# A bias added by a matmul, routing placed ahead of gate 2 on TensorE, and GpSimd splitting three of four weight quarters

## Chip, core and metric

One core of a Trainium2 chip runs the whole kernel. The metric is device time in microseconds of one launch. The kernel before took 1426.2 us (median of 3 runs, 1423.9 to 1431.74).

## What is computed

One layer of an encoder with 256 tokens of width 2048, all in float32. Its weights are read once: 539 MB in all. Cut to its steps:

```python
c_act = jax.nn.silu(c)
mod = c_act @ w_ada[l] + b_ada[l]
sh1, sc1, g1, sh2, sc2, g2 = [m[:, None, :] for m in jnp.split(mod, 6, axis=-1)]
h = rms_norm(x, g_mix[l]) * (1 + sc1) + sh1
y = token_mixer(h, w_in[l], ..., w_out[l])      # gMLP, pooling, attention; ends with @ w_out
x = x + g1 * y
h = rms_norm(x, g_ffn[l]) * (1 + sc2) + sh2
x = x + g2 * moe_ffn(h, w_router, b_router, e_gate[l], e_up[l], e_down[l])

def moe_ffn(h, ...):                            # 16 experts, top-1 group, top-2 experts
    eidx, gw = route(ht, w_router, b_router)
    order = jnp.argsort(flat_e)                 # tokens sorted by expert
    hid = jax.nn.silu(xb @ w_gate[e]) * (xb @ w_up[e])
    return hid @ w_down[e]                      # weighted by the gate, summed per token
```

## The kernel before

The program is written as one list of steps, without a scheduler: each engine runs its instructions in the order in which they stand in the code, and waits only for the data and buffers that it needs.

**Stages.** First come the mixer's projections. `w_in` is taken in five chunks of rows (`CHUNKS`; the last three have four blocks of 128 rows), each chunk in nine pieces of 512 columns. Then 16 tiles of `w_out` in four column groups `n` (`wout_steps`, `x1_block`). Then the routing of the tokens, the gather of the normalised tokens into `XT` (16 blocks, four matmuls each), and the experts, 15 of which are visited in `ORDER`, with 8 tiles of `e_gu` and 4 of `e_down` for each, 2 MB a tile.

**Loads.** All weights come through SyncE's DMA queue (SP) into a ring of four 2 MB tiles (`ring` three times, `ringm`), which are used as eight halves of 1 MB until the experts begin. Two more (`ringl`) take the place of the buffers `xhl` and `oneh` when the gather has read them (`s_phl.close()`). SP issues in the order of the code; a load waits for the last reader of its buffer.

**Splitting.** A quarter of a `w_in` or `w_out` tile (128x512) is split into a high part, which ScalarE casts, and a low part, which VectorE ("V") or GpSimd ("G") computes by a subtraction (`split`, L176). `WSPLIT` and `WSO` name the engine of each quarter. TensorE then takes six matmuls for a quarter (`mm3` for each half of the tokens), the third of which is the first to need the low part. Up to six quarters lie ready (`LOOK_SPLITS`).

**Modulation rows.** A row such as gate 2 (`g2`, section 5 of `w_ada`) is computed in four parts of 512 columns. Each part takes four 1 MB tiles; `ada_parts` accumulates them on TensorE in rows 0, 32, 64 and 96 of one PSUM bank (`accs[0]`), four matmuls a tile. A step waits in the list `todo`, so its load is issued some steps ahead of its matmuls (`LOOK` = 4, a gate-2 step counts 2). At the end of a part `gate_row` copies the bank to `r2[q]` on ScalarE (L795) and adds the bias in one row on VectorE (L797). Of the 16 gate-2 steps five are issued among the last `w_out` tiles (`G2`), one behind them (`G2_MID`), and the others by two calls of `g2_run`: one ahead of the routing's counts, one behind the matmul that gives the experts' order.

**Routing.** `M` marks the two experts of each token (L1050). `pp` holds the sums over tokens, by matmuls of `M` (L1056 to L1061). From them VectorE makes `key`, a rank, and the one-hot `ohc`; the matmul `po` (L1087) turns it into the order of the experts; `irow` (L1091) is that order as integers. SP reads `irow` before it can issue the first expert's load (L1352). `x_lo` (L1004) is the low part of the normalised tokens, four instructions of VectorE that the gather needs but the order doesn't. `oneh` (L1118) is the one-hot matrix by which the gather's matmuls sort the tokens. `g2w` (L1187 to L1190) spreads gate 2 over all partitions, by four matmuls with `sel`; the expert stage needs it.

## Time and profile before

| | |
|---|---|
| time, three runs | 1423.9, 1426.2, 1431.74 us |
| profiled execution | 1423.43 us, span 1421.7 us, mean granted TensorE clock 0.959 |
| TensorE matmul (PE) busy | 1202.6 us, 85% of the span, 6638 instructions |
| VectorE (DVE) busy | 628.1 us, 44%, 1168 |
| ScalarE (ACT) busy | 363.7 us, 26%, 661 |
| GpSimd (POOL) busy | 161.1 us, 11%, 127 |
| DMA | 539.13 MB, mean 379 GB/s |

Times in the views count from the start of the span. PE is TensorE's matmul row and PEld its weight loads; matmuls overlap in the records, so the distance from one start to the next tells their rate, and the recorded length of a single one does not. A float32 matmul stands as two instructions. The granted clock is given as a share of 2.4 GHz: 0.50 is the lower level, 1.2 GHz. "Idle before" in brackets names what ended an engine's wait. The time beyond the span, 1423.43 - 1421.7 = 1.7 us, is the same start and end in every run and is left as it is.

### The profile page before, as it was taken

To read this page: it belongs to the slowest core of one execution; us is meant where nothing else is said; L and a number is where in the kernel's file an instruction comes from. 1 tells how busy PE (TensorE), PEld (TensorE's weight loads), DVE (VectorE), ACT (ScalarE), POOL (GpSimd) and SP (SyncE) were. 2 spreads that over 40 slices of the span, in tenths; PEclk is the share of its full clock that TensorE was granted. 3 is DMA by queue.
4 is the path that set the end of the run, shared out by engine and by line. 5 is a ranking of instruction groups with operands and counts; after the bars stand their busy time and mean duration, and the time that the engine had idled before them with its cause. 6 is when DMAs were issued, how large, how long until landed. Compare 5 with 4: busy or idle time off the path is not lost.

```text
span 1421.7 us, 17020 instructions
## 1 busy us (share of the span) xinstructions
PE 1202.6 (85%) x6638; PEld 625.6 (44%) x6638; DVE 628.1 (44%) x1168; ACT 363.7 (26%) x661; POOL 161.1 (11%) x127
## 2 busy tenths in 40 slices
PE   5998999999899686899968999688885888858865
PEld 3665676665676252664325743322232222322221
DVE  4366585765786463893327951121130211302112
ACT  4543334535444240771005820000000000000000
POOL 1333433321444000000000000000000000000000
PEclk9999999999999888999989999999998999989988
DMA  9888686899979489998999989999999999999997
GB/s 391 355 349 317 248 349 228 322 342 354 366 293 379 176 355 428 426 427 334 427 426 427 427 331 429 426 427 427 426 427 426 427 427 427 426 426 427 427 427 291
DMA packets 49222, 539.13 MB, mean 379 GB/s; under 512 B 5472, under 2 KB 5600, under 8 KB 7024
## 3 DMA queue, kind: packets, MB, share of 16 engines
q1 hardware_dynamic: 47664, 534.79, 91.6%
q10 hardware_dynamic: 1472, 3.19, 0.6%
q8 instruction: 54, 0.88, 0.2%
q14 instruction: 32, 0.26, 0.1%
HBM read 535.86 MB, written 2.10 MB: 378 GB/s over the span
## 4 chain that ended last, share of the span: by engine, by line
PE 33%; DMA 33%; DVE 2%; ACT 1%; issue 1%; DVEq 0%; ACTq 0%
PE lbank L171 24%; DMA ring<-in_e_down_dram 14%; DMA ring<-in_e_gu_dram 9%; DMA ringm<-in_e_gu_dram 6%; PE bank L171 4%; PE pm L171 3%; PE ada L171 2%; DMA ringl<-in_e_down_dram 2%; DMA ringl<-in_e_gu_dram 2%; DVE el L176 0%; DVE xhl L1004 0%; ACT xhl L998 0%; ACT el L175 0%; PE pt L171 0%; PE pt L892 0%
## 5 line engine op out<-in xcount | busy, mean ns | idle before, releaser
L171 PE MATMUL pm<-whl,hT 128*128 128x512 f32 x1056 | 283.2, 404 | 6.6 <-ACT whl L175 3.8
L171 PEld LDWEIGHTS pm<-whl,hT 128*128 128x128 f32 x1056 | 198.5, 192 | 78.7 <-issue 13.6
L171 PE MATMUL lbank<-ring,xr 128*32 128x256 f32 (+1 forms) x1216 | 155.4, 494 | 41.3 <-DMA ring<-in_e_gu_dram 41.3
L176 POOL TENSOR_TENSOR whl<-ring,whl 128x512 fp32r<-128x512 f32 x86 | 120.7, 1415 | 221.5 <-ACT whl L175 207.2
L171 PE MATMUL bank<-y,gt 128*128 128x512 f32 x240 | 119.9, 623 | 0.0
L175 ACT CAST whl<-ring 128x512 fp32r<-128x512 f32 x172 | 99.5, 621 | 64.8 <-PE pm L171 52.3
L1344 DVE TENSOR_TENSOR xa<-xa,bank 128x512 f32<-128x512 f32 x120 | 82.5, 688 | 73.6 <-PE bank L171 73.6
L171 PEld LDWEIGHTS lbank<-ring,xr 128*32 128x32 f32 (+1 forms) x1216 | 55.2, 127 | 133.6 <-issue 63.4
L1335 DVE TENSOR_TENSOR y<-lbank,g2w 128x512 f32<-128x512 f32 x60 | 41.5, 691 | 157.4 <-PE lbank L171 157.4
L171 PE MATMUL lbank<-ring,hidT 128*64 128x512 f32 (+1 forms) x416 | 81.7, 683 | 30.8 <-DVE hidT L1303 15.8
L171 PE MATMUL lbank<-ringl,xr 128*32 128x256 f32 (+1 forms) x608 | 80.3, 511 | 31.9 <-DMA ringl<-in_e_gu_dram 31.9
L176 DVE TENSOR_TENSOR whl<-ring,whl 128x512 fp32r<-128x512 f32 x86 | 84.6, 999 | 35.2 <-ACT whl L175 34.9
L171 PE MATMUL lbank<-el,xs 128*128 128x512 f32 x384 | 91.2, 395 | 7.3 <-ACT el L175 5.5
L1285 DVE TENSOR_TENSOR hid<-hid,lbank 128x512 f32<-128x512 f32 x11 | 7.6, 687 | 202.0 <-PE lbank L171 201.8
L171 PE MATMUL lbank<-ringm,xr 128*32 128x256 f32 (+1 forms) x608 | 78.4, 494 | 21.6 <-DMA ringm<-in_e_gu_dram 20.9
L1231 ACT COPY gt<-bank 128x256 f32<-128x256 f32 x15 | 5.6, 372 | 338.2 <-PE bank L1229 338.2
L171 PE MATMUL ada<-ring,cact 128*1 128x512 f32 (+1 forms) x568 | 70.4, 599 | 21.7 <-DMA ring<-in_w_ada_dram 13.1
L171 PEld LDWEIGHTS lbank<-el,xs 128*128 128x128 f32 x384 | 71.3, 188 | 27.4 <-ACT el L175 7.6
L171 PE MATMUL lbank<-ringl,hidT 128*64 128x512 f32 (+1 forms) x416 | 74.2, 598 | 4.7 <-DMA ringl<-in_e_down_dram 4.7
L171 PEld LDWEIGHTS bank<-y,gt 128*128 128x128 f32 x240 | 42.1, 193 | 73.3 <-issue 70.9
L454 DVE TENSOR_TENSOR z<-z,pm 128x512 f32<-128x512 f32 x72 | 48.5, 685 | 57.5 <-PE pm L171 57.5
L1280 DVE TENSOR_TENSOR hid<-hid,lbank 128x256 f32<-128x256 f32 x6 | 2.5, 421 | 158.8 <-PE lbank L171 136.3
(385 smaller groups left out, 1214.1 us busy)
## 6 DMA issues: line engine op xcount, KB each, us to landing
ring<-in_e_gu_dram SPq DMA_DIRECT2D x60, 2048.0 KB
ring<-in_w_ada_dram SPq DMA_DIRECT2D x79, 1024.0 KB, 6.9
ringm<-in_e_gu_dram SPq DMA_DIRECT2D x30, 2048.0 KB, 25.7
ringl<-in_e_gu_dram SPq DMA_DIRECT2D x30, 2048.0 KB, 24.9
ring<-in_e_down_dram SPq DMA_DIRECT2D x30, 2048.0 KB, 24.3
ringl<-in_e_down_dram SPq DMA_DIRECT2D x30, 2048.0 KB
ring<-in_w_in_dram SPq DMA_DIRECT2D x30, 1024.0 KB, 9.9
ring<-in_w_out_dram SPq DMA_DIRECT2D x12, 1024.0 KB, 7.9
```

The costliest lines, as they stand in the source:

```text
L171: E.matmul(out, lhsT=lhsT, rhs=rhs, start=start, stop=stop, skip_group_check=True)
L175: S.copy(hi, src)
L176: (eng or V).tensor_tensor(lo, src, hi.bitcast(F32), op=OP.subtract)
L454: V.tensor_tensor(dst, dst, P[h], op=OP.add)
L1231: S.copy(gt, p[:, :256])
L1280: V.tensor_tensor(hid[:, :256], hid[:, :256], P[1][:, :256], op=OP.mult)
L1285: V.tensor_tensor(hid[:, o], hid[:, o], P[2 * b + 1], op=OP.mult)
L1335: V.tensor_tensor(y, P, g2w[:, c0:c0 + 512], op=OP.mult)
L1344: V.tensor_tensor(a, a, p, op=OP.add)
```

## The change

Five edits belong together:

- The bias of gate 2 is added by a matmul: `bgt`, an 8x512 tile of both gates' biases, is multiplied with a one-hot column into row 0 of the part's bank. The part then ends with ScalarE's copy alone. The bias rows come by one DMA from ScalarE's queue in place of eight.
- The four parts of gate 2 alternate between `accs[0]` and `sets[0][0]`, a bank that the last column group of `w_out` doesn't use. The banks of `w_out` are named by `sets` in place of the rotation.
- Of the ten last gate-2 steps four, not eight, are issued ahead of the routing's counts. The other six, with the copies and `g2w`, come behind `oneh` in the code and ahead of the gather.
- One of the four `x_lo` stands ahead of `key`, and three behind `irow` (before: two and two).
- In the chunks 2, 3 and 4 of `w_in` and in `w_out` GpSimd splits the quarters 0, 2 and 3 and VectorE quarter 1 (before: V, G, V, G).

```diff
--- before.py
+++ after.py
@@ -64,10 +64,10 @@
 
 LAST = ["mwm", "mwm", "mw", "mawmam", "amw", "mmmwammm", "ammam", "ammammgmx", "amvammm", "aamsmapmtmmmm"]
 
-G2, G2_MID, NG2 = [1, 2, 1, 1], 1, 2
+G2, G2_MID, NG2 = [1, 2, 1, 1], 1, 4
 
 M1A, M1B, M2A, M2B, G1 = "PPVV", "PPPP", "PPPP", "PPPP", "PVVV"
-WSPLIT, WSO = ["VGVG"] * 5, "VGVG"
+WSPLIT, WSO = ["VGVG", "VGVG", "GVGG", "GVGG", "GVGG"], "GVGG"
 NORM = "GV"
 
 
@@ -255,8 +255,8 @@
         load_tile(w, wada_d, ADA[sec, k0, g])
         return w.rearrange("p (k n) -> p k n", n=n)
 
-    def ada_parts(sec, k0, nk, after, acc):
-        P = accs[acc]
+    def ada_parts(sec, k0, nk, after, acc, bias=None):
+        P = accs[acc] if isinstance(acc, int) else acc
         r = 16 // nk
         ng = KD // r
 
@@ -267,7 +267,10 @@
             def run(w):
                 for j in range(r):
                     k, t = r * g + j, j % 4
-                    mm(P[32 * t:32 * t + 1, :128 * nk], cact[:, k:k + 1], w[:, j, :], start=k < 4, stop=k >= KD - 4)
+                    mm(P[32 * t:32 * t + 1, :128 * nk], cact[:, k:k + 1], w[:, j, :], start=k < 4,
+                       stop=k >= KD - 4 and (t > 0 or bias is None))
+                if g == ng - 1 and bias is not None:
+                    mm(P[0:1, :], ident[0:8, bias:bias + 1], bgt, start=False)
                 if g == ng - 1:
                     after(P)
             return prep, run
@@ -791,13 +794,9 @@
     ss1 = cst.tile([128, 2, 4], F32, name="ss1")
     lnj = cst.tile([128, 1], F32, name="lnj")
 
-    def gate_row(sec, q, out, P):
+    def gate_row(out, P):
         S.copy(out, P)
-        o = slice(32 * q, 32 * q + 1)
-        V.tensor_tensor(out[o, :], out[o, :], bgr[o, sec // 3, :], op=OP.add)
-
-    def gate_args(sec, q, out):
-        return sec, 4 * q, 4, lambda P: gate_row(sec, q, out, P), 0
+        V.tensor_tensor(out[0:1, :], out[0:1, :], bgt[0:1, :], op=OP.add)
 
     wr = par("wr").rearrange("p (k e) -> p k e", e=16)
     wra = wk2.tile([128, KD, 16], F32, name="wra", bufs=1)
@@ -815,10 +814,8 @@
 
 
     rt, s_rt = pool("rt")
-    bgr = rt.tile([128, 2, 512], F32, name="bgr")
-    for q in range(4):
-        for a in range(2):
-            nc.scalar.dma_start(bgr[32 * q:32 * q + 1, a, :], bg_d[a:a + 1, 512 * q:512 * q + 512])
+    bgt = rt.tile([8, 512], F32, name="bgt2")
+    nc.scalar.dma_start(bgt, bg_d.rearrange("a (q n) -> (a q) n", n=512))
 
     def rtile(shape, name):
         return rt.tile(shape, F32, name=name)
@@ -857,7 +854,7 @@
     def wout_steps(n, Ps):
         def banks():
             if not Ps:
-                Ps.extend([pm(), pm()])
+                Ps.extend(sets[n % 2])
             return Ps
 
         def one(g):
@@ -907,7 +904,7 @@
 
     def g1_bc(n):
         p = pt()
-        mm(p, sel if n == 0 or G1[n] == "P" else ones, r4s[n])
+        mm(p, sel if n == 0 else ones, r4s[n])
         g1 = wk2.tile([128, 512], F32, name="g1")
         S.copy(g1, p)
         return g1
@@ -921,10 +918,8 @@
     def g1_steps(n):
         r4s.append(grow())
         if n == 0:
-            gate_row(2, 0, r4s[0], g1_first[0])
+            gate_row(r4s[0], g1_first[0])
             return []
-        if G1[n] == "P":
-            return steps(ada_parts(*gate_args(2, n, r4s[n])))
         return steps(sum_parts(2, 4 * n, 4, lambda a: None, 0, ENG(G1[n]), lambda: r4s[n], n))
 
     r4s = []
@@ -939,6 +934,7 @@
 
     g1_load(1)
     pbanks.append(accs[1])
+    sets = [list(pbanks)[:2], list(pbanks)[2:]]
     r2, g2p, g1s = [], deque(), {}
 
     def g2_run(n):
@@ -955,7 +951,8 @@
             if n == 3 and g == 0:
                 r2 += [grow2() for _ in range(4)]
                 for q in range(4):
-                    g2p.extend(ada_parts(*gate_args(5, q, r2[q])))
+                    g2p.extend(ada_parts(5, 4 * q, 4, lambda P, q=q: S.copy(r2[q], P), (accs[0], sets[0][0])[q % 2],
+                                         4 + q))
             if n == 3:
                 for _ in range(G2[g]):
                     step(*g2p.popleft())
@@ -1050,7 +1047,7 @@
     V.tensor_tensor(M, oh1, oh2, op=OP.add)
 
 
-    g2_run(len(g2p) - NG2)
+    g2_run(NG2)
     pp = pt()
     for h in range(2):
         mm(pp[:, 32:48], one2, M[:, h, :], h == 0, h == 1)
@@ -1059,7 +1056,7 @@
     mm(pp[:, 0:16], stri2, M[:, 0, :])
     mm(pp[:, 16:32], stri2, M[:, 1, :], stop=False)
     mm(pp[:, 16:32], one2, M[:, 0, :], start=False)
-    x_lo(2)
+    x_lo(1)
     SQ = [128, 16, 16]
     tmp = rtile(SQ, "tmp")
 
@@ -1085,11 +1082,9 @@
     V.tensor_scalar(ohc, ioE[0:16, 0, :], rkc[:, 16:17], None, op0=OP.is_equal)
     po = pt()
     mm(po[:, 0:16], ec.to_broadcast([16, 128]), ohc)
-    g2_run(16)
-    flush()
     irow = cst.tile([1, 128], I32, name="irow")
     V.tensor_copy(irow[:, 0:16], po[0:1, 0:16])
-    x_lo(2)
+    x_lo(3)
     order = rtile([128, 16], "order")
     V.tensor_copy(order, po[:, 0:16])
     pos = rtile([128, 3, 16], "pos")
@@ -1118,6 +1113,13 @@
         V.scalar_tensor_tensor(oneh[:, h, :], io512, sl2[:, 1, h:h + 1], oneh[:, h, :].bitcast(F32),
                                op0=OP.is_equal, op1=OP.add)
 
+    g2_run(16)
+    flush()
+
+    for b in range(4):
+        p = pm()
+        mm(p, sel, r2[b])
+        S.copy(g2w[:, 512 * b:512 * b + 512], p)
     def gather(k):
 
         p = pm()
@@ -1183,11 +1185,6 @@
         pick(gatO[:, h, :], ohO, gatR[:, h, :])
         V.tensor_tensor(posR[:, h, :], posR[:, h, :], dlt, op=OP.add)
 
-
-    for b in range(4):
-        p = pm()
-        mm(p, sel, r2[b])
-        S.copy(g2w[:, 512 * b:512 * b + 512], p)
     s_phl.close()
     pl, s_pl = pool("pl", 1, side="right")
     wides += [pl.tile([128, 2 * RINGW], F32, name=f"ringl{i}") for i in range(RING_LAST)]
```

The order of the loads on SP's queue is the same in both kernels. On GpSimd the number of split instructions grows from 104 to 147, and on VectorE it falls from 104 to 61: 27 tiles of `w_in` and 16 of `w_out`, one quarter each.

TensorE before, from the two tiles that stand ahead of `M`'s matmuls to the last gate-2 tile (`ada_113` is `accs[0]`, `pt_122` is `pp`, `pt_123` is `po`):

```order
L171 MATMUL ada_113<-ring_64,cact 1x512 x8
L171 MATMUL ada_113<-ring_65,cact 1x512 x4
L171 MATMUL ada_113<-ringm_2677,cact 1x512 x8
L171 MATMUL pt_122<-M,one_2710 128x16 x2
L171 MATMUL pt_122<-one_2710,M 16x1 x2
L171 MATMUL pt_122<-M,stri_2712 128x16 x2
L171 MATMUL pt_122<-M,one_2710 128x16
L171 MATMUL pt_123<-ohc,ec 128x16
L171 MATMUL ada_113<-ring_65,cact 1x512 x4
L171 MATMUL ada_113<-ring_63,cact 1x512 x8
L171 MATMUL ada_113<-ring_64,cact 1x512 x4
```

TensorE in the changed kernel at the same place (`pm_120` is `sets[0][0]`):

```order
L171 MATMUL pm_120<-ring_64,cact 1x512 x4
L171 MATMUL pm_120<-bgt_2689,ident 1x512
L171 MATMUL pt_122<-M,one_2703 128x16 x2
L171 MATMUL pt_122<-one_2703,M 16x1 x2
L171 MATMUL pt_122<-M,stri_2705 128x16 x2
L171 MATMUL pt_122<-M,one_2703 128x16
L171 MATMUL pt_123<-ohc,ec 128x16
L171 MATMUL ada_113<-ring_64,cact 1x512 x4
L171 MATMUL ada_113<-ring_65,cact 1x512 x4
L171 MATMUL ada_113<-ringm_2677,cact 1x512 x8
L171 MATMUL ada_113<-bgt_2689,ident 1x512
L171 MATMUL pm_120<-ring_65,cact 1x512 x4
```

Five tiles (20 matmuls) stood ahead of `pp` here, and now one; behind `po` there are eight tiles in place of four, and each part ends with a matmul of `bgt`.

TensorE before, at the end of the gather and the first expert's tile:

```order
L171 MATMUL pm_119<-oneh,xhl 128x512 x4
L171 MATMUL ada_114<-oneh,xhl 128x512 x4
L171 MATMUL pm_120<-grow_3327,sel 128x512
L171 MATMUL pm_121<-grow_3328,sel 128x512
L171 MATMUL pm_119<-grow_3329,sel 128x512
L171 MATMUL ada_114<-grow_3330,sel 128x512
L171 MATMUL lbank<-ringm_2677,xr_3910 32x256 x16
```

TensorE in the changed kernel, from the end of gate 2 to the first blocks of the gather:

```order
L171 MATMUL pm_120<-ring_64,cact 1x512 x4
L171 MATMUL pm_120<-bgt_2689,ident 1x512
L171 MATMUL pm_120<-grow_3320,sel 128x512
L171 MATMUL pm_121<-grow_3321,sel 128x512
L171 MATMUL pm_119<-grow_3322,sel 128x512
L171 MATMUL ada_114<-grow_3323,sel 128x512
L171 MATMUL pm_120<-oneh,xhl 128x512 x4
L171 MATMUL pm_121<-oneh,xhl 128x512 x4
```

The four matmuls of `g2w` stood between the gather and the first expert, and now stand ahead of the gather.

VectorE before, from `M` to the second pair of `x_lo` (`grow` is a row of `r2`, `xhl` is written by `x_lo`):

```order
L1050 TENSOR_TENSOR M<-oh_3608,oh_3615 128x32
L797 TENSOR_TENSOR grow_3328<-grow_3328,bgr 1x512
L797 TENSOR_TENSOR grow_3329<-grow_3329,bgr 1x512
L1004 SCALAR_TENSOR_TENSOR xhl<-xa,rs_3530,xhl 128x1024 x2
L1079 SCALAR_TENSOR_TENSOR key<-pt_122,rev 128x16
L1080 SCALAR_TENSOR_TENSOR keyc<-pt_122,revc 16x1
L1082 TENSOR_SCALAR rkc<-key,keyc 16x16
L1083 TENSOR_REDUCE rkc<-rkc 16x1
L1085 TENSOR_SCALAR ohc<-ioE,rkc 16x16
L797 TENSOR_TENSOR grow_3330<-grow_3330,bgr 1x512
L1091 CAST irow<-pt_123 1x16
L1004 SCALAR_TENSOR_TENSOR xhl<-xa,rs_3530,xhl 128x1024 x2
```

VectorE in the changed kernel:

```order
L1047 TENSOR_TENSOR M<-oh_3601,oh_3608 128x32
L1001 SCALAR_TENSOR_TENSOR xhl<-xa,rs_3523,xhl 128x1024
L1076 SCALAR_TENSOR_TENSOR key<-pt_122,rev 128x16
L1077 SCALAR_TENSOR_TENSOR keyc<-pt_122,revc 16x1
L1079 TENSOR_SCALAR rkc<-key,keyc 16x16
L1080 TENSOR_REDUCE rkc<-rkc 16x1
L1082 TENSOR_SCALAR ohc<-ioE,rkc 16x16
L1086 CAST irow<-pt_123 1x16
L1001 SCALAR_TENSOR_TENSOR xhl<-xa,rs_3523,xhl 128x1024 x3
```

Two bias additions left the way from `M` to `key`, and one left the place ahead of `irow`; one `x_lo` moved behind it.

## Rows read from the trace of the kernel before

**Rows 1.** Windows: length, busy of PE, PEld, DVE, ACT, POOL (counts), clock, DMA share, GB/s.
```profile
482.30:497.00 14.70, 9.01 (x68) 3.04 (x60) 5.57 (x11) 1.17 (x2) 0.00 (x0) 0.88 0.02 7
...
518.00:521.50 3.50, 3.50 (x16) 2.82 (x15) 3.04 (x11) 3.00 (x5) 0.00 (x0) 1.00 0.10 42
521.50:569.70 48.20, 35.25 (x344) 13.87 (x342) 13.00 (x26) 5.03 (x8) 0.00 (x0) 0.89 0.99 411
569.70:705.00 135.30, 126.62 (x527) 74.04 (x528) 82.61 (x137) 61.84 (x103) 0.00 (x0) 1.00 0.97 402
```

**Rows 2.** Chain that ended last, in order of time: start, length, what, count.
```profile
479.45 4.96 PE ada L171 x32
...
485.75 2.48 DVE xhl L1004 x2
489.12 0.60 PE pt L171 x2
489.73 4.90 PE ada L171 x32
494.65 0.59 ACT grow L795
495.27 0.69 DVE grow L797
...
517.71 2.72 PE pm L171 x12
...
521.33 2.58 PE pm L171 x6
```

**Rows 3.** Timeline of the routing and the first expert loads: start, length, instruction, idle before.
```profile
479.45 3.19 PE L171 MATMUL ada<-ring,cact 128*1 128x512 f32 x16 [3.00 <-ACT grow L795]
480.38 0.19 DVE L1050 TENSOR_TENSOR M<-oh,oh 128x32 f32<-128x32 f32 x1
484.28 0.62 PE L171 MATMUL pt<-M,one 128*128 128x16 f32 x4
485.48 0.38 PE L171 MATMUL pt<-M,one 128*128 128x16 f32 x2
488.14 0.17 DVE L1079 SCALAR_TENSOR_TENSOR key<-pt,rev 128x16 f32<-128x16 f32 x1
495.99 0.16 DVE L1091 CAST irow<-pt 1x16 int32<-1x16 f32 x1
496.97 0.35 SPq L1352 DMA_DIRECT2D ringm<-in_e_gu_dram  x1
503.80 5.73 PE L171 MATMUL pm<-oneh,xhl 128*128 128x512 f32 x12 [9.22 <-DVE oneh L1118]
521.45 0.87 SPq L1352 DMA_DIRECT2D ringl<-in_e_gu_dram  x2
```

**Rows 4.** Windows of TensorE alone: length, PE busy, granted clock, DMA share, GB/s.
```profile
489.60:491.00 1.40, 1.40 (x9) 0.50 0.04 12
...
492.40:494.60 2.20, 2.18 (x21) 1.00 0.00 0
```

**Rows 5.** Timeline at the first `w_out` tile: bias loads, ScalarE's first copy, TensorE's first matmul.
```profile
358.99 2.37 ACTq L821 DMA_DIRECT2D bgr<-in_bg_dram  x8
...
361.39 0.58 ACT L795 COPY grow<-ada 128x512 f32<-128x512 f32 x1 [4.15 <-DVE capR L850]
...
362.55 0.75 PE L171 MATMUL pm<-whl,hT 128*128 128x512 f32 x1 [3.19 <-ACT whl L175]
```

**Rows 6.** Splits by engine (min/median/max ns), TensorE's waits 135 to 467, one window.
```profile
L176 DVE TENSOR_TENSOR whl<-ring,whl x86: 671/693/1789, 24.2 to 448.0; 128x512 fp32r<-128x512 f32 x86
L176 POOL TENSOR_TENSOR whl<-ring,whl x86: 1268/1294/1817, 24.8 to 449.2; 128x512 fp32r<-128x512 f32 x86
...
PE pm L171 <- ACT whl L175: 3.4, 2, 3.2
PE pt L412 <- DVE hf L414: 2.1, 3, 0.9
...
375.00:440.00 65.00, 64.52 (x323) 50.56 (x322) 57.19 (x73) 27.56 (x54) 29.30 (x22) 1.00 0.87 342
```

## The prediction

> **What bounds the kernel now.** I read the windows by stage first, to see which resource sets the pace where. From 521.5 us the DMA engines are busy for 0.99 of the time [rows 1]: the first expert waits for weights. Then TensorE sets the pace (126.6 of 135.3 us in 569.7 to 705, while DMA still has a share of 0.97 there, since the ring stays full). So behind 521.5 everything hangs on when the stream of expert weights starts and is not stopped again. Ahead of it there are two gaps in that stream: 14.7 us from 482.3 to 497.0, with a share of 0.02, and 3.5 us from 518.0 to 521.5 with 0.10 [rows 1]. The reader is to see that no engine is full in the first gap: TensorE is busy 9.0, VectorE 5.6 of 14.7 us. It is a chain of waits, and I read the chain next [rows 2]: TensorE's gate 2 (479.45), VectorE's low parts (485.75), the matmul `po` (489.12), gate 2 again (489.73), ScalarE's copy (494.65), VectorE's bias (495.27). Only behind that bias does VectorE write `irow`, at 495.99, and SP issues the first expert's load at 496.97 [rows 3]. The second gap ends when the gather has read `xhl` and SP can load into `ringl`, at 521.45 [rows 3]. In the mixer ahead of it TensorE is nearly full (64.5 of 65 us in 375 to 440 [rows 6]), so what the change does there is a matter of a microsecond or two.
>
> **The order of the experts.** `M` is ready at 480.38 + 0.19 = 480.57 [rows 3]. Its matmuls `pp` start at 484.28, as two gate-2 tiles that start at 479.45 and two more stand ahead of them on TensorE. In the change only two tiles and a bias matmul stand there. Those two tiles were done before the idle 3.00 us that end at 479.45 [rows 3], so at 476.45. The trace has no matmul of 8 rows by one column; the nearest is a `g2w` matmul with the same 512 columns, three of which take 2.58, so 0.86 [rows 2], or 1.72 at half clock. Even that ends at 478.2, ahead of `M`. So `pp` starts at 480.57, takes what it took (484.28 to 485.48 + 0.38: 1.58) and ends at 482.15. VectorE does one `x_lo` meanwhile (2.48 / 2 = 1.24 [rows 2], to 481.81). From `key` to `po` it took 489.12 - 488.14 = 0.98 [rows 2, 3], `po` itself 0.60: `po` ends at 483.73. `irow` no longer stands behind the last bias: 0.16 of its own [rows 3], with an allowance of 0.05 for the signal, make 483.95, where it was 496.15. That is 12.2 us sooner, but the stream does not win all of it.
>
> **The gate-2 tiles behind it.** The first expert load now waits for its buffer. It goes to `ringm`, whose two halves hold the third and fourth of the eight tiles that TensorE now takes behind `po`. Four tiles behind `po` took 4.90 us [rows 2], the first part at half clock and the rest at full: the window shows 0.50 up to 491.0 and 1.00 from 492.4 [rows 4]. I take 4.90 for the first four again, as TensorE comes from a lull here too: 488.63, and the load at 488.9, against 496.97. That is 8.0 us sooner. The bytes are there: DMA was idle from 482.3 on [rows 1], with all gate-2 loads landed, and SP's order is the same. The other four tiles go at full clock, 21 instructions in 2.18 us [rows 4], eight a tile: 0.83 each, 3.3. Two biases add 2 x 0.86 = 1.7: gate 2 ends at 493.7.
>
> **`g2w` and the gather.** `g2w` waits for the last part's copy (0.59 [rows 2]) since its first bank is the one being copied; what stands behind it, the gather, waits too. It starts at 494.3 and takes 4 x 0.86 = 3.4: 497.7. `oneh` is no longer what the gather waits for. Before, it came 503.80 - 495.99 = 7.8 after `irow` began [rows 3], with two `x_lo` between; with three it is 9.05 after 483.8, 492.8. The gather's full rate is 12 instructions in 2.72 us [rows 2], so 64 take 14.5: it ends at 512.2. Before, it ended where `g2w` began, 521.33 [rows 2], after 17.5 us, the first of them slow. Now TensorE comes into it straight from work, so I take the full rate. SP follows 0.1 behind: 512.3 against 521.45 [rows 3]. The first four loads took 21 us (497.0 to 518.0 [rows 1]); from 488.9 they end at 509.9, so the second gap remains, 2.4 us long, and the stream behind it starts **9.1 us sooner**. `g2w` no longer stands between the gather and the first expert's matmuls, which gives TensorE 3.4 us more; that costs and brings nothing, as DMA sets the pace there [rows 1]. This cover fails only if TensorE came more than 9.1 us late, and it comes about 11 sooner.
>
> The bounds: if TensorE stayed at half clock through all eight tiles, they would cost 1.60 each (16 instructions in 3.19 [rows 3]) and the biases 1.72, 16.2 in place of 9.9, and the gain falls to 2.8. If the whole ran at full clock, 1.6 more are won. I take the middle case, which is what the same instructions did before.
>
> **The mixer.** At the first `w_out` tile ScalarE issues eight bias loads in 2.37 us ahead of its copy, and TensorE waits 3.19 us for the first cast [rows 5]. One load in place of eight saves 7/8 of 2.37 = 2.1. The first quarter's low part comes from GpSimd, 1.29 against 0.69 [rows 6], 0.6 later. Net gain 1.4, bounds 0 (the cast waits for something else, as the releaser in rows 5 says) and 3.2 (the whole wait). One bias matmul falls into the full stretch ahead of 467 and costs 0.86. For the 43 splits moved to GpSimd I take nothing: TensorE's waits from 135 to 467 are 11.9 us in all (3.4 and 2.1 the longest of ten groups [rows 6]), which bounds a gain, and GpSimd has room. In 375 to 440, some 10 tiles, it is busy for 29.3 of 65 us; ten splits of 1.29 to 1.82 more make 42 to 48. The cover is the six quarters that lie ready. Mixer in all: 1.4 - 0.9 = **0.5 us sooner**.
>
> A rule is to be weighed here. VectorE's split takes 0.69 in the median but up to 1.79, and GpSimd's 1.29 but up to 1.82 [rows 6]: 1.79 is less than 0.69 + 1.29, 1.82 less than 1.29 + 0.69. The Trainium skill ("SBUF — State Buffer", section "Who interferes with whom") says that a VectorE instruction with two SBUF inputs and a GpSimd one that reads SBUF exclude each other, and the second waits for the whole of the first. The trace agrees in size. By that rule a tile holds the shared port for 3 x 1.29 + 0.69 = 4.56 us, where it was 3.96; ten tiles make 45.6 of 65 us, so the sum stays as it is.
>
> **The sum.** 9.1 + 0.5 = 9.6: the profiled execution's 1423.4 would be 1413.8. It lies 2.8 below the median of the runs, 1426.2, off which the same gain gives 1416.6. I forecast **1416**.
>
> **The rivals.**
> 1. *TensorE stays slow.* With only small matmuls between 478 and 484 the clock stays down through gate 2. For it: behind the lull that ends at 489.6 it stands at 0.50 [rows 4], and in the change TensorE has a longer one. Against: it rose within four tiles at 489.7. Gain 2.8 + 0.5 = 3.3: 1423.
> 2. *GpSimd sets the pace of the splits*: slower than before. Place: `w_out` and the last three chunks, 43 tiles; each tile has 24 matmuls of 0.227, 5.45 us. GpSimd needs 3 splits and, in `w_out`, 0.3 us of additions a tile. It decides when a split takes on average over 1.72 us in `w_out`. At the longest seen, 1.82, 16 tiles lose 0.3 each, 5 us: 1421. To end slower by 0.5% it must eat the 9.6 and 7.1 more, 16.7 over 43 tiles: about 2 us a split. For it: splits wait on each other up to 1.8. Against: the median is 1.29 and VectorE's share falls. At 2.05 the time is 1433.
> 3. *The stream's start is hidden anyway.* TensorE's stretch from 569.7 would not start sooner, as something else holds it. Against: DMA is at 0.99 up to there [rows 1]. Then only the mixer's 0.5 are left: 1426.
> 4. *More than the sum*: full clock all through and the whole wait at `w_out`, and some of VectorE's waits gone: 9.6 + 1.6 + 1.8 + 1: 14, 1412.
>
> **How the numbers follow.** Runs of this kernel spread over 8 us, so 0.5% (7.1 us) is about what can be told from no change. My sum, 7.1 to 12 us gained: 0.58. Case 4: 0.10. Case 1, or the sum short by over 2.5 us: 0.17. Case 2 with a small loss: 0.06; with a large one 0.04. Case 3: 0.05. Faster: 0.58 + 0.10 = 0.68; slower 0.04; same 0.28. The range goes from 1409 (case 4, and a run at the low end) to 1424 (case 1), which leaves out case 3 and the large loss.
>
> **What the profile would show.** Right: `irow` at about 484 and the first `e_gu` load about 5 us behind it, waiting for TensorE's gate 2 rather than for VectorE; the gap near 482 about 7 us long in place of 14.7; the gather without a wait for `oneh`, 14.5 us long; `ringl` loaded near 512. The experts' stage as long as before. GpSimd's splits 147, with a median near 1.3 us and TensorE's waits for them under 2 us. Wrong: a granted clock of 0.50 through the eight tiles; waits of TensorE on GpSimd's `whl` in `w_out`; a `ringl` load that comes late for another reason, or a longer experts' stage.

## The result, and the profile after

The changed kernel takes 1418.35 us (median of 5 runs, 1417.67 to 1421.07), the kernel before 1429.06 in the same comparison (5 runs, 1423.9 to 1431.74): a ratio of 0.9935, 95% interval 0.991 to 0.9959, or 9.3 us faster (5.9 to 12.9). Compared once more, with 11 runs against 28, it was 0.9942 (0.9923 to 0.9961). The prediction, 1416 in a range of 1409 to 1424, held. Its parts held less well than their sum.

The profiled execution of the changed kernel is its longest run (1421.07 us, span 1419.3), and that of before (1423.43) is shorter than each of the five runs of before, so the spans differ by 2.4 us only. The stages are compared from mark to mark instead.

The timeline of the routing after the change; columns as in [rows 3]:

```profile
478.36 0.19 DVE L1047 TENSOR_TENSOR M<-oh,oh 128x32 f32<-128x32 f32 x1
478.61 1.03 PE L171 MATMUL pt<-M,one 128*128 128x16 f32 x4 [3.76 <-DVE M L1047]
480.64 0.59 PE L171 MATMUL pt<-M,one 128*128 128x16 f32 x2
...
482.79 3.59 PE L171 MATMUL ada<-ring,cact 128*1 128x512 f32 x16
...
482.90 0.16 DVE L1086 CAST irow<-pt 1x16 int32<-1x16 f32 x1 [0.69 <-PE pt L171]
489.07 1.01 PE L171 MATMUL ada<-bgt,ident 8*1 8x512 f32 x2
489.21 0.35 SPq L1349 DMA_DIRECT2D ringm<-in_e_gu_dram  x1
490.01 3.61 PE L171 MATMUL pm<-ring,cact 128*1 128x512 f32 x32
...
495.25 2.84 PE L171 MATMUL pm<-grow,sel 128*128 128x512 f32 x6 [0.67 <-ACT grow L954]
498.38 3.33 PE L171 MATMUL pm<-oneh,xhl 128*128 128x512 f32 x12
513.62 0.87 SPq L1349 DMA_DIRECT2D ringl<-in_e_gu_dram  x2
```

Counted from `M`, `irow` comes after 4.5 us (482.90 - 478.36) where it took 15.6 [rows 3], and no bias of VectorE stands ahead of it. The first expert load comes 10.9 us behind `M` (16.6 before) and waits, as predicted, for the fourth gate-2 tile, not for `irow`. The gather starts without a wait for `oneh`. The `ringl` load comes 35.3 us behind `M`, 41.1 before: 5.8 us won, not the 9.1 of the prediction.

The windows of the two gaps in the stream of weights and of the first experts, columns as in [rows 1]:

```profile
482.30:489.20 6.90, 6.90 (x35) 1.52 (x36) 6.17 (x12) 0.00 (x0) 0.00 (x0) 0.56 0.01 2
510.50:513.60 3.10, 3.00 (x14) 2.15 (x12) 0.01 (x1) 2.60 (x5) 0.00 (x0) 1.00 0.04 16
513.60:561.90 48.30, 32.30 (x336) 12.70 (x336) 13.09 (x26) 2.75 (x4) 0.00 (x0) 0.89 0.99 412
```

The first gap shrank from 14.7 us to 6.9 [rows 1], and TensorE is now full in it. The second is 3.1 us, where it was 3.5: it was bound to stay, since the four loads that come first end sooner too.

TensorE's own windows behind `M`, columns as in [rows 4]:

```profile
478.60:481.30 2.70, 2.62 (x14) 0.50 0.40 170
482.80:486.10 3.30, 3.30 (x17) 0.50 0.02 5
486.10:489.10 3.00, 3.00 (x21) 0.63 0.00 0
489.10:491.00 1.90, 1.90 (x18) 1.00 0.65 129
```

After the idle 3.76 us ahead of `pp` the granted clock is at its lower level (0.50) through `pp`, `po` and most of the first four tiles. Before, `pp` came straight out of gate-2 tiles and ran at the higher level (1.58 us against 2.62 here), as the window of before shows:

```profile
484.00:486.00 2.00, 1.86 (x18) 1.00 0.00 0
```

The start of the output projection; its counterpart is [rows 5]:

```profile
356.57 0.30 ACTq L818 DMA_DIRECT2D bgt<-in_bg_dram  x1
358.17 0.50 PE L171 MATMUL pm<-whl,hT 128*128 128x512 f32 x1 [1.22 <-ACT whl L175]
358.40 1.42 DVE L842 TENSOR_TENSOR triE<-ioE,ioR 128x256 f32<-128x256 f32 x1
359.59 0.73 PE L171 MATMUL pm<-whl,hT 128*128 128x512 f32 x2 [0.69 <-POOL whl L176]
359.90 1.11 DVE L850 TENSOR_SCALAR limR<-capR 128x16 f32<-128x16 f32 x1
361.06 1.69 DVE L799 TENSOR_TENSOR grow<-grow,bgt 1x512 f32<-1x512 f32 x1
362.68 0.67 DVE L176 TENSOR_TENSOR whl<-ring,whl 128x512 fp32r<-128x512 f32 x1
363.40 0.74 PE L171 MATMUL pm<-whl,hT 128*128 128x512 f32 x2 [2.16 <-DVE whl L176]
```

One bias load in place of eight cut the wait for the first cast from 3.19 to 1.22 us. But two new waits stand behind it, 0.69 and 2.16: VectorE's quarter comes at 362.68 only, behind three small instructions that take 4.22 us together. So the start of the projection is no shorter than it was: 4.07 us of waits against 3.19, and the first matmul of the second `w_out` tile comes 13.2 us behind the mark "entry" of the table below, 13.3 before. The clock makes up for the longer waits: before, it was 0.50 to 0.53 from 362.5 to 366.0, behind the one wait of 3.19 us, and here it stays at 1.00 from 358.1 to 367.0.

The splits by engine, and the page's line of busy times; counterparts in [rows 6] and in the table of the profile before:

```profile
L176 POOL TENSOR_TENSOR whl<-ring,whl x121: 1261/1293/2341, 25.9 to 447.1; 128x512 fp32r<-128x512 f32 x121
...
L176 DVE TENSOR_TENSOR whl<-ring,whl x51: 671/851/1768, 25.4 to 442.5; 128x512 fp32r<-128x512 f32 x51
```

```profile
PE 1203.5 (85%) x6646; PEld 624.8 (44%) x6646; DVE 592.9 (42%) x1121; ACT 364.1 (26%) x661; POOL 217.4 (15%) x170
```

GpSimd works 56.3 us more, VectorE 35.2 less.

### The profile page after: what moved, and what is told of

It is laid out like the page before. It is cut to its first block, busy times and chain, and to the rows that moved or that the text cites. A ratio compares the mean times of both kernels' runs of the same rounds, so it can differ in the third digit from the quotient of the medians.

```text
span 1419.3 us, 17046 instructions
## 1 busy us (share of the span) xinstructions
PE 1203.5 (85%) x6646; PEld 624.8 (44%) x6646; DVE 592.9 (42%) x1121; ACT 364.1 (26%) x661; POOL 217.4 (15%) x170
## 3 DMA queue, kind: packets, MB, share of 16 engines
q10 hardware_dynamic: 1472, 3.19, 0.6%
## 4 chain that ended last, share of the span: by engine, by line
PE 53%; DMA 37%; DVE 4%; issue 2%; ACT 2%; POOL 1%; SPq 0%; DVEq 0%; POOLq 0%; ACTq 0%
PE lbank L171 22%; PE pm L171 19%; DMA ring<-in_e_down_dram 15%; DMA ring<-in_e_gu_dram 11%; DMA ringm<-in_e_gu_dram 6%; PE ada L171 6%; PE bank L171 3%; DMA ringl<-in_e_down_dram 2%; DMA ringl<-in_e_gu_dram 2%; PE pt L171 2%; DMA ring<-in_w_ada_dram 1%; POOL whl L176 1%; DVE el L176 0%; DVE hf L417 0%; DVE z L457 0%
## 5 line engine op out<-in xcount | busy, mean ns | idle before, releaser
L171 PE MATMUL pm<-whl,hT 128*128 128x512 f32 x1056 | 279.7, 401 | 8.1 <-DVE whl L176 4.3
L171 PEld LDWEIGHTS pm<-whl,hT 128*128 128x128 f32 x1056 | 197.6, 191 | 77.4 <-issue 12.8
L176 POOL TENSOR_TENSOR whl<-ring,whl 128x512 fp32r<-128x512 f32 x121 | 166.5, 1394 | 182.8 <-ACT whl L175 178.0
L171 PE MATMUL lbank<-ring,xr 128*32 128x256 f32 (+1 forms) x1216 | 152.5, 482 | 37.2 <-DMA ring<-in_e_gu_dram 37.2
L171 PE MATMUL lbank<-ring,hidT 128*64 128x512 f32 (+1 forms) x416 | 84.5, 713 | 31.4 <-DMA ring<-in_e_down_dram 16.7
L171 PE MATMUL ada<-ring,cact 128*1 128x512 f32 (+1 forms) x504 | 61.5, 589 | 18.1 <-DMA ring<-in_w_ada_dram 13.1
L176 DVE TENSOR_TENSOR whl<-ring,whl 128x512 fp32r<-128x512 f32 x51 | 50.3, 990 | 44.3 <-ACT whl L175 44.2
```

Of the source, the lines that this page charges most:

```text
L171: E.matmul(out, lhsT=lhsT, rhs=rhs, start=start, stop=stop, skip_group_check=True)
L176: (eng or V).tensor_tensor(lo, src, hi.bitcast(F32), op=OP.subtract)
```

## Experiments

Each was compared with the kernel before, run on the same chip between its own runs. "Gain" is one minus the ratio, times before's median there (1427.89 us for the first four, 1425.08 for the next four, 1429.88 for the last four). A diff is against the kernel that the text names.

**Only the splits moved** (the kernel before with one line of the change):

```diff
-WSPLIT, WSO = ["VGVG"] * 5, "VGVG"
+WSPLIT, WSO = ["VGVG", "VGVG", "GVGG", "GVGG", "GVGG"], "GVGG"
```

> The kernel before with the last part of the change alone: GpSimd splits three of four quarters in the chunks 2 to 4 and in w_out. Theory (the gain is in the routing's chain of waits): no change, 0 us with 2 either way; a stretch ahead of w_out may be quicker by 2 us, and the first w_out tiles slower by 2 to 3, since GpSimd's run of splits makes VectorE's instructions with two SBUF inputs wait. Rival (unloading VectorE brings a share of the gain): 3 us or more faster, with the instant at which M is ready (480.6 us before) at 478 or sooner.

Measured: 1425.46 us (12 runs), ratio 0.999 (0.9974 to 1.0006): no change that can be told. `M` comes at 480.64, where it was 480.38.

**The change without the splits** (the changed kernel, that line taken back):

> The changed kernel with the splits as before (V, G, V, G). Theory: all of the gain, 9 to 11 us faster than the kernel before, with the first expert load about 8 us and the ringl load about 8 us sooner than in the kernel before; at the first w_out tile TensorE waits less than in the changed kernel, where it waited 4.1 us in three pieces. Rival (splits carry a share): 6 us or less.

Measured: 1421.23 us, ratio 0.9946 (0.993 to 0.9962), a gain of 7.7 us, between the theory and its rival. From `M` to the `ringl` load 34.4 us (35.3 with the splits). At the first `w_out` tile TensorE waits 4.7 us (1.22 and 3.51), and not less than with the splits, as expected.

**Bias by matmul and the second bank, the order as before** (the change without `NG2`, the places of `x_lo`, `g2_run` and `g2w`, and the splits; only the line that names bias and bank is shown, against the kernel before):

```diff
-                    g2p.extend(ada_parts(*gate_args(5, q, r2[q])))
+                    g2p.extend(ada_parts(5, 4 * q, 4, lambda P, q=q: S.copy(r2[q], P), (accs[0], sets[0][0])[q % 2],
+                                         4 + q))
```

> The kernel before with the bias of gate 2 by a matmul, two banks in turn and one bias load; the order of the gate-2 steps, of the low parts x_lo and of g2w as before, splits as before. Theory: the order is not what wins; what counts is that irow stands behind no bias addition and the second pair of tiles behind no copy. Worked out on the rows of before: pp at 483.6, irow at 487.0 in place of 496.2, first expert load at 487.9, gather from 494.6 to about 510.5, ringl load at 510.6 in place of 521.45: 10.9 us sooner, and 1 us at the first w_out tile, so 10 to 13 us faster, no less than the changed kernel. Rival (the order is what wins): 4 us or less, with irow later than 490.

Measured: 1419.06 us, ratio 0.9931 (0.9916 to 0.9947), a gain of 9.9 us: the whole of what the change brings, in the old order.

**The new order and the second bank, the bias on VectorE** (the changed kernel, splits as before; the lines that load `bgr` are left out):

```diff
...
+    def gate2_row(q, out, P):
+        S.copy(out, P)
+        o = slice(32 * q, 32 * q + 1)
+        V.tensor_tensor(out[o, :], out[o, :], bgr[o, :], op=OP.add)
...
-                    g2p.extend(ada_parts(5, 4 * q, 4, lambda P, q=q: S.copy(r2[q], P), (accs[0], sets[0][0])[q % 2],
-                                         4 + q))
+                    g2p.extend(ada_parts(5, 4 * q, 4, lambda P, q=q: gate2_row(q, r2[q], P), (accs[0], sets[0][0])[q % 2]))
```

> The changed kernel's order and two banks, but the bias of gate 2 is added on VectorE as before, and the splits are as before. Theory: in this order the additions of the last two parts stand behind oneh and cost the path nothing; VectorE's tail behind oneh ends 3 us later, still under the gather. So as fast as the changed kernel without its splits, within 1.5 us: 8 to 10 us faster than before. Rival (VectorE must be free of gate 2): at least 3 us slower than that.

Measured: 1418.75 us, ratio 0.9936 (0.9919 to 0.9953), a gain of 9.1 us. With the new order VectorE needn't be free of gate 2: its last two additions stand behind `oneh` (496.68), where nothing of the routing waits for them.

Both versions have the second bank, so it was taken apart further.

**The bias by matmul alone** (one bank, order and splits as before; the diff is against the version with bias and bank):

```diff
-                    g2p.extend(ada_parts(5, 4 * q, 4, lambda P, q=q: S.copy(r2[q], P), (accs[0], sets[0][0])[q % 2],
+                    g2p.extend(ada_parts(5, 4 * q, 4, lambda P, q=q: S.copy(r2[q], P), accs[0],
```

> The kernel before, with the biases of the second gate added by matmul (one bias load, no bias add on VectorE for it), the four quarters still in one accumulator bank one after the other, order and splits as before. Theory: in the version with both the bank and the bias changed VectorE waits for nothing of gate 2 and irow stands 7.2 us behind M (15.6 before); with one bank TensorE waits again for ScalarE's copy of each quarter (3.0 us once before), but no longer for an add on VectorE behind the routing; irow at 8 to 11 us behind M, and 4 to 8 us below before. Rival: the bank is what counts, and this version stays within 3 us of before.

Measured: 1422.66 us (12 runs), ratio 0.9959 (0.9945 to 0.9974), a gain of 5.9 us. TensorE waits for the one bank's copy, and four tiles (two entries of 16 instructions) and a bias matmul stand between that wait and `pp`; the timeline of this run:

```profile
484.82 3.59 PE L171 MATMUL ada<-ring,cact 128*1 128x512 f32 x16 [0.68 <-ACT grow L954]
485.74 0.19 DVE L1047 TENSOR_TENSOR M<-oh,oh 128x32 f32<-128x32 f32 x1
488.18 2.95 PE L171 MATMUL ada<-ringm,cact 128*1 128x512 f32 x16
492.01 0.62 PE L171 MATMUL pt<-M,one 128*128 128x16 f32 x4
```

`pp` stands 6.3 us behind `M` (492.01 - 485.74), later than the 3.9 of before, and `irow` still comes after 9.5 in place of 15.6, as the theory had it (8 to 11): what was won lies behind `pp`.

**The second bank alone** (the kernel before, the banks of the projection named by `sets` as in the change):

```diff
-                    g2p.extend(ada_parts(*gate_args(5, q, r2[q])))
+                    g2p.extend(ada_parts(5, 4 * q, 4, lambda P, q=q: gate_row(5, q, r2[q], P), (accs[0], sets[0][0])[q % 2]))
```

> The kernel before, with the quarters of the second gate going to two accumulator banks in turn; bias adds on VectorE, eight bias loads, order and splits as before. Theory: the second bank takes TensorE's 3.0 us wait for ScalarE's copy away, but the routing's chain on VectorE still has the quarters' adds in it, and an add waits for its quarter's copy, so irow stays 11 to 14 us behind M; 2 to 5 us below before. Rival: the adds on VectorE cost nothing (as with the changed order), and the bank alone brings all 9 us.

Measured: 1424.17 us (12 runs), ratio 0.9968 (0.9953 to 0.9983), a gain of 4.6 us. VectorE's queue in this run:

```profile
482.09 0.19 DVE L1051 TENSOR_TENSOR M<-oh,oh 128x32 f32<-128x32 f32 x1
...
494.05 0.69 DVE L797 TENSOR_TENSOR grow<-grow,bgr 1x512 f32<-1x512 f32 x1 [7.03 <-ACT grow L795]
494.77 0.16 DVE L1092 CAST irow<-pt 1x16 int32<-1x16 f32 x1
```

`pp` comes at once, but `irow` still waits 7.03 us behind a bias whose copy is late: 12.7 us behind `M`. So the two causes are separate, the bank ahead of `pp` and the bias ahead of `irow`, and their gains add within the noise: 4.6 and 5.9 alone on one chip, 9.9 together on another; from `M` to the `ringl` load 2.5 and 6.7 us alone, 9.4 together.

**`g2w` behind the gather again** (the changed kernel):

```diff
     flush()
-
-    for b in range(4):
-        p = pm()
-        mm(p, sel, r2[b])
-        S.copy(g2w[:, 512 * b:512 * b + 512], p)
     def gather(k):
...
+    for b in range(4):
+        p = pm()
+        mm(p, sel, r2[b])
+        S.copy(g2w[:, 512 * b:512 * b + 512], p)
     s_phl.close()
```

> The changed kernel, with the four selector matmuls of g2w and their copies put behind the gather again, as before the change. Theory: what ends the routing stage is the load into ringl, which waits for the gather's last readers; in the changed kernel the g2w block holds TensorE from 495.25 to 498.38, so that with it moved the gather begins about 3 us sooner, the ringl load comes at about 510.5 instead of 513.6, the first expert matmul hardly sooner (g2w now stands between), and the median is 2 to 3 us below that of the changed kernel, about 11 to 12 us below before. Rival: the first round of experts is paced by the loads that were already issued at 489, so an earlier ringl load changes nothing and the medians agree within 1 us. Second rival: the gather then waits for VectorE's one-hot rows (ready at 492.8), which takes nothing, since gate 2 ends at 494.6.

Measured: 1414.75 us, ratio 0.992 (0.99 to 0.9941). The gather starts 17.0 us behind `M` (20.0 in the changed kernel), the `ringl` load 31.9 (35.3). That is a gain of 11.4 us over before; the 2 to 3 us beyond the changed kernel's 9.3 and 8.3 lie inside the intervals.

**And six tiles ahead of `pp`** (the last kernel with one more line):

```diff
-G2, G2_MID, NG2 = [1, 2, 1, 1], 1, 4
+G2, G2_MID, NG2 = [1, 2, 1, 1], 1, 6
```

> As the run before in this call, and six instead of four tiles of gate 2 run ahead of M's matmuls. Theory: TensorE sits idle for 3.76 us ahead of those matmuls in the changed kernel (474.85 to 478.61), and two more tiles (1.9 to 3.6 us each pair) fit there, so that they no longer stand between the routing and the gather: ringl load at about 508, 2 to 3 us sooner than with four tiles, unless VectorE's one-hot rows (492.8) become what the gather waits for; then only about 1 us. The clock in that stretch should stay high (granted 0.81 in 467 to 485 of the changed kernel), so M's matmuls take 1.6 us instead of 2.6. Median 1 to 3 us below the other. Rival: two tiles take longer than the idle time and delay M's matmuls and irow by 1 to 2 us, which gives the gain back; no difference.

Measured: 1413.9 us, ratio 0.9913 (0.9894 to 0.9933). TensorE's idle time ahead of `pp` falls to 1.93 us, `pp` runs at the higher clock (478.21 to 479.78), and the `ringl` load comes 27.8 us behind `M`, 4.2 sooner than in the run before it. The time is only 0.9 us lower (1 to 3 were expected), which these intervals don't tell from nothing.

**The same two edits with the bias on VectorE**: no new line, they are put into the version with the new order and the bank.

> The changed order with the bias of gate 2 added on VectorE (eight one-row adds), two banks, splits on two engines in turn as before; with g2w behind the gather and six tiles ahead of M's matmuls. Theory: the same gain as the version with the bias by matmul, minus nothing for VectorE's four adds, which come behind the one-hot rows; ringl load about 4 us sooner than in the same kernel with four tiles and g2w ahead (515.05 there), median 2 to 4 us below the changed kernel. Rival: the four adds wait behind the one-hot rows and hold g2w, whose matmuls now stand behind the gather, so nothing is held; if the adds instead came in front of one-hot rows, the gather would be late by their 4 x 0.7 us.

Measured: 1415.28 us, ratio 0.9923 (0.9904 to 0.9943); the gather waits 1.16 and 0.39 us for `oneh`.

**Four small instructions moved out of the start of the output projection** (the changed kernel):

```diff
+    def late_consts():
+        V.tensor_tensor(r4s[0][0:1, :], r4s[0][0:1, :], bgt[0:1, :], op=OP.add)
+        V.tensor_scalar(revc, ec, -1.0, 16.0, op0=OP.mult, op1=OP.add)
+        V.tensor_tensor(triE, ioE, ioR, op=OP.is_lt)
+        V.tensor_scalar(limR, capR, -1.0, 512.0, op0=OP.mult, op1=OP.add)
...
+            if n == 0 and g == 1:
+                then(late_consts)
```

> The changed kernel, with four small VectorE instructions taken out of the start of the output projection and put behind its second weight tile: the bias add on the first row of gate 1 (1.69 us there), triE (1.42), limR (1.11) and revc (0.14). Theory: the wait that the change moved (TensorE 2.16 us for VectorE's quarter at 363.40) is made by these, since VectorE's first split stands behind them; with them gone it falls below 0.5 us, and M comes 2 us sooner; put later they cost what they cost without a run of GpSimd's splits beside them, or what that run makes of them, and delay at most one quarter there. Median 1 to 2 us below the changed kernel. Rival: the wait is not VectorE's queue but the weights (the ring tile's own load, or ScalarE's rounding), so TensorE waits as long for something else and the time stays within 1 us.

Measured: 1413.5 us, ratio 0.9913 (0.9893 to 0.9933). The wait of 2.16 us is gone:

```profile
358.70 0.50 PE L171 MATMUL pm<-whl,hT 128*128 128x512 f32 x1 [1.22 <-ACT whl L175]
359.04 0.40 PE L171 MATMUL pm<-whl,ylo 128*128 128x512 f32 x1
360.12 0.73 PE L171 MATMUL pm<-whl,hT 128*128 128x512 f32 x2 [0.69 <-POOL whl L176]
360.69 0.39 PE L171 MATMUL pm<-whl,ylo 128*128 128x512 f32 x1
360.92 0.62 PE L171 MATMUL pm<-whl,hT 128*128 128x512 f32 x2
361.38 0.39 PE L171 MATMUL pm<-whl,ylo 128*128 128x512 f32 x1
```

No third wait follows, and the projection (marks of the table below) takes 115.0 us in place of 117.5. The gain over before is 12.4 us, more than the theory had; the intervals of this ratio and the changed kernel's still overlap.

**All three edits together, and the changed kernel on the same chip**: the lines of the last edits in one kernel (`g2w` behind the gather, `NG2` 6, the small instructions late).

> The changed kernel with the three edits that helped put together: four small VectorE instructions behind the second weight tile of the output projection, g2w behind the gather, six tiles of gate 2 ahead of M's matmuls. Theory: the first edit ends TensorE's 2.2 us wait at the output projection, the other two bring the ringl load forward by 6 to 7 us against M; they lie in different stages, so the gains add: 3 to 5 us below the changed kernel that runs in this call. Rival: the expert stage gives an earlier start of the weight loads back, since between 560 and 700 us TensorE and the splits set the pace and the ring is full (GB/s in 562 to 650 fell from 408 before to 390 after, 383 with the earliest start so far), so that what is gained ahead of the first expert is worth under half; then no more than 3 us below.

> The changed kernel as it stands, for a comparison on one chip with the others of this call. Theory: about 9 us below the kernel before (ratio 0.9935 as measured first). Rival: the first result leaned on three of five runs of before that were long; then the ratio here is nearer 0.997.

Measured: 1410.5 us, ratio 0.988 (0.9856 to 0.9903), 17.2 us below before; the changed kernel in the same comparison 1421.12 us (11 runs, 1416.26 to 1424.99), ratio 0.9942. The difference of the ratios makes 8.9 us, more than the 3 to 5 expected. This is the best version here; a part of that difference may lie in the wide spread of the changed kernel's runs there.

The marks of all 14 profiled executions, in us. "Entry" is the last pair of matmuls ahead of the output projection (`pm<-ident,z`), "proj" from there to the matmul `pt<-sel,x1T`, "irow", "gather" and "ringl" count from the start of `M`, "experts" runs from the `ringl` load to the last addition to `xa`, and "rest" from there to the end of the span.

```
                       entry   proj      M   irow gather ringl experts rest
before                356.40 117.08 480.38  15.61  23.42 41.07  893.19  7.1
changed kernel        353.98 117.48 478.36   4.54  20.02 35.26  896.02  9.7
changed kernel again  351.37 117.47 475.75   4.52  20.03 35.25  894.84  9.7
only the splits       354.79 118.96 480.64  15.67  23.48 41.17  893.65  6.5
without the splits    357.73 120.12 484.75   4.53  19.14 34.38  896.17  7.9
bias + bank           357.49 120.10 484.49   7.23  14.94 31.71  895.46  7.9
order + bank          356.12 119.12 482.13   4.59  17.71 32.92  895.34  7.0
bias alone            357.73 121.10 485.74   9.51  17.22 34.34  893.26  8.6
bank alone            356.78 118.40 482.09  12.68  20.50 38.59  896.94  7.0
g2w behind            355.39 117.48 479.77   4.54  16.96 31.92  897.85  9.5
  and six tiles       353.57 117.49 477.96   3.27  12.84 27.75  898.16  9.4
  bias on VectorE     357.16 119.41 483.47   4.59  13.49 29.05  897.68  7.0
small ones late       354.51 115.02 476.42   4.54  19.61 34.84  893.30  6.4
all three             352.61 115.04 474.55   3.48  15.85 30.82  896.62  6.4
```

## Why the prediction was right, and where it was not

**The stream of weights starts sooner and the time follows.** This is the prediction's main step, and it is shown: the gain comes with the `ringl` mark, and in the kernels that shorten only the way to it, with the splits as before, the time falls (bias alone, bank alone, both, order). Rival 3, that the start is hidden anyway, falls with it. Order and size are two things, though. On the profiles' own clock the `ringl` load comes 0.8 us sooner than before with the bank alone (520.68 for 521.45) and 1.4 with the bias alone (520.08), as `M` comes later there, and the medians fall by 4.6 and 5.9; in the changed kernel it is 7.8 us against 9.3, with six tiles 15.7 against 12.4. The profiled run of before lies near the low end of its runs (1422.0 to 1432.9), and where the longer ones spend their time stands in no trace. So some 4 us of the first two gains are in none of the marks.

**The order of the experts.** `irow` was predicted 3.6 us behind `M` (483.95 - 480.38) and came after 4.5. The 1.0 us is `pp` at the lower clock. That `M`'s matmuls would take what they had taken was the step that failed: TensorE now stood idle in front of them, and the prediction had counted that lull (476.45 to 480.57) only as room. With six tiles the idle time is 1.93 us and `pp` takes 1.57 at the higher clock. The length of the idle time is not all that counts: in the kernel without the splits it is 2.06 us and `pp` takes 2.62 at the lower clock, but there the two tiles ahead of it already ran at 0.50 (480 to 482), where in the changed kernel and with six tiles the clock was high until the lull.

**The gate-2 tiles.** The first four were put at the 4.90 us of [rows 2] and took 6.28 (482.79 to 489.07), since the clock rose only near their end; with `pp` this makes the first load 2.3 us later behind `M` than predicted (10.85 against 8.5). Eight tiles and two biases took 11.8 us (482.79 to 494.61) and not 9.9. That lies between the prediction's case (full clock soon) and its rival 1 (16.2), 1.9 us from the one and 4.4 from the other. `g2w` took 3.1 for 3.4 and the gather 15.0 for 14.5. Together the `ringl` load lies 35.3 us behind `M` where 31.9 was predicted: the term of 9.1 us measured 5.8.

**The mixer.** The term of 0.5 us measured 2.0 at `M`, and two of its parts were wrong, the 1.4 for the bias loads and the nothing for the splits. The bias loads bring nothing: the 2.0 us saved at the first cast are lost again by the second tile, with the waits for GpSimd's and VectorE's quarters, and the stage takes 117.5 us, before 117.1. Without the splits one load is worse still (120.1): the bias load is issued at 360.32, VectorE stands at the addition until it lands, and its quarter of the first tile stands behind that, for which TensorE waits 3.51 us:

```profile
364.65 0.85 DVE L799 TENSOR_TENSOR grow<-grow,bgt 1x512 f32<-1x512 f32 x1 [0.89 <-DMA bgt<-in_bg_dram]
...
366.16 1.22 PE L171 MATMUL pm<-whl,hT 128*128 128x512 f32 x2 [3.51 <-DVE whl L176]
```

The splits, put at nothing, bring some 3 us up to the entry of the projection: the seven profiles with three quarters on GpSimd enter it at 351.4 to 355.4, mean 353.8, the seven with two at 356.1 to 357.7, mean 357.1. Alone they lose 1.9 us again in the projection, behind the eight bias loads, and so no time was won by them alone. Where in the chunks the 3 us arise was not followed up.

**GpSimd as the bound (rival 2)** didn't come: its median split stays 1.29 us, and TensorE's waits for it from 135 to 467 us sum to 1.4. The rival's price was wrong by its own terms: 16.7 us are lost at 1.91 us a split, and 2.05 would lose 35.

**What is given back.** The prediction let the experts' stage be as long as before. In the changed kernel it is 2.8 us longer, 1.7 in the second profile. Over the table, the seven profiles with a `ringl` load at 513.62 or sooner have a stage of 896.4 us in the mean, the five with one at 519 or later 894.6, each with a scatter of 2 (the two between them 895.4). Windows from 600 to 650 us, of before and of the changed kernel, columns as in [rows 1]:

```profile
600.00:650.00 50.00, 45.56 (x192) 34.78 (x192) 45.09 (x74) 37.56 (x62) 0.00 (x0) 1.00 0.95 394
```

```profile
600.00:650.00 50.00, 45.55 (x188) 32.38 (x188) 41.34 (x68) 31.91 (x53) 0.00 (x0) 1.00 0.89 362
```

TensorE is as full as before (45.6 of 50 us) and the loads run slower, at 362 GB/s for 394: buffers come free at TensorE's pace there, so a stream that is ahead has to wait. That fits a gain that is partly given back, and the six-tile run, where 4.2 us more at `ringl` brought 0.9; no run here takes that stage apart, so it is argued, not shown.

**The sum.** That 9.1 + 0.5 came out is in part luck: one term was 3.3 us too large and the other 1.5 too small, and the runs of before are longer in the median than the profiled one, for which the sum was made. In the profile 7.8 us are won at the `ringl` load, 5.0 at the last addition to `xa` and 2.4 at the end of the span. The rest of the span was 7.1 us before and 9.7 after; it ranges from 6.4 to 9.7 over the kernels, 9.4 to 9.7 in four profiles with the changed start and 6.4 in the two with the small instructions moved. It isn't the output: the packets of its last store end 3.9 us behind the start of that addition before and 4.0 after. What follows are the semaphore instructions that close the program, and in the four profiles with 9.4 to 9.7 us, and in no other, TensorE's queue stands for 3.0 to 3.2 us between two of them (from 4.6 to 7.7 us behind the addition in the changed kernel). Why it stands there is open.

**The change itself** is more than is needed. Bank and bias, or bank and order, bring its whole gain; the one that is left adds nothing that can be measured. The order without the bank was not tried.

## What to carry to other kernels

An instruction that nobody urgent waits for costs what stands behind it in its engine's queue: here an addition of 0.7 us that waited for its copy held an order for which a whole stream of loads waited, and, with the second bank, it was enough to move either it or what stood behind it. Idle time that is made ahead of a chain of small matmuls isn't free room: put work of the same engine there, or price what follows at the lower clock. When a wait is removed, look for the next late thing on the other engines' queues (here VectorE's constants) before the saved time is counted.

## What the runs showed of the hardware

Small VectorE instructions took as long as what was left of GpSimd's split beside them. GpSimd's first split at the start of the projection, its third and fourth together, and its fourth, in windows that cut its run into pieces:

```profile
358.27 1.26 POOL L176 TENSOR_TENSOR whl<-ring,whl 128x512 fp32r<-128x512 f32 x1
```

```profile
360.94 3.57 POOL L176 TENSOR_TENSOR whl<-ring,whl 128x512 fp32r<-128x512 f32 x2
```

```profile
362.16 2.34 POOL L176 TENSOR_TENSOR whl<-ring,whl 128x512 fp32r<-128x512 f32 x1
```

The first ends at 359.53, and `triE` (0.40 us before) at 359.82; the second ends by 360.94, where the third starts, and `limR` (0.18 before) at 361.01; the third ends by 362.2, and the bias (0.68 before) at 362.75. The fourth takes 2.34 us and has VectorE's quarter (362.68 to 363.35) in its first half. So each engine in turn waits for an instruction of the other: 1.26 us of VectorE's work became 4.22. The Trainium skill ("SBUF — State Buffer", section "Who interferes with whom") says that a VectorE instruction with two SBUF inputs and a GpSimd one that reads SBUF exclude each other, for the whole of the first, and counts `tensor_scalar` among those that can take the shared ports; the trace agrees on both, for `limR` has one input and waited (it took 0.15 in the run with the small ones late). What wasn't expected is that it counts most where VectorE's instructions are shortest: a run of GpSimd's splits makes each cost up to one of them.

The clock after the same lull wasn't the same in two kernels. With six tiles ahead TensorE's order behind `M` is the same in the runs "g2w behind and six tiles" and "all three"; windows of TensorE alone, first of the one, then of the other:

```profile
484.00:486.00 2.00, 2.00 (x11) 0.87 0.58 115
```

```profile
484.00:486.00 2.00, 2.00 (x16) 0.50 0.94 401
```

In the one the clock rises in a window that begins 6.0 us behind `M`; in the other it is still at the lower level in one that begins 9.5 us behind it. That is why the gather starts at 15.9 us there and not at 12.8. What differs, the loads that run beside it or the instant at which `M` falls, was not told apart.
